# Forgetting attention: row maxima from a product with the queries in rows, subtracted inside the score product

## The chip, the cores and the metric

The kernel runs on one core of a Trainium2 chip. The metric is the device time of one execution in microseconds (us). TensorE (PE in the profile) multiplies matrices, VectorE (DVE) and ScalarE (ACT) work on elements, GpSimd (POOL) does a few fills, and SyncE (SP) issues the DMAs. TensorE writes to PSUM, in which the kernel keeps eight tiles ("banks" below) of 128 x 512 fp32; the other data lie in SBUF.

## The reference

One decoder layer on 2048 tokens of width 1024, in fp32: adaLN modulation, a combined input projection, sliding-window attention on 8 heads, forgetting attention on 8 heads of 64, an output projection, a gated MLP of width 2816 with a causal convolution, and a final norm. The change touches the forgetting attention:

```python
def forgetting_attention(q, k, v, f_logit):
    F = jnp.cumsum(jax.nn.log_sigmoid(f_logit.astype(jnp.float32)), axis=1)
    ...
    def one_block(args):
        qi, Fi, n = args
        s = jnp.einsum('bqhd,bkhd->bhqk', qi, k).astype(jnp.float32) * (HEAD_DIM ** -0.5)
        s = s + (Fi[..., None] - Fk[:, :, None, :])
        q_pos = n * BLOCK + jnp.arange(BLOCK)
        s = jnp.where(k_pos[None, :] <= q_pos[:, None], s, NEG)
        p = jax.nn.softmax(s, axis=-1)
        return jnp.einsum('bhqk,bkhd->bqhd', p.astype(v.dtype), v)
```

Each query has its own shift (the row maximum) in the softmax; any shift gives the same result as long as the exponentials stay in range.

## The kernel before

**Numbers.** A fp32 operand is split into a high part, rounded to the type fp32r that TensorE multiplies fast, and a low part that holds the rest. A dense product is three matmuls (high x high, high x low, low x high).

**Stages.** The tokens are cut into four blocks n = 0..3 of 512. For each block s1 projects the input, s2 does both attentions, and s3 does the output projection and the MLP. s2 is a side stream: `merge` weaves it into a main stream of dense products (s2(0) into s1(1) and s1(2); s2(1) into s3(0); s2(2) into s1(3) and s3(1); s2(3) into s3(2)); s3(3) is alone. Both streams yield costs in the planner's own microseconds; the side stream advances when its sum of costs lies behind the main one's, times a ratio (`RM`, `att_cost`), and when the last step lies far enough back (`GAPS`, `SGAPS`). Within what they write, a scheduler then orders each engine's queue. The engines take their queues in order.

**Forgetting attention before (`fox`, `fox_unit`).** Scores lie transposed: 128 keys in the partitions, queries in the columns. A unit is one head and 512 queries (blocks 0 and 1) or 256 queries (blocks 2 and 3: two key blocks then share a 512-column tile). `score` makes two matmuls for each key block: the stationary operand holds the keys' high and low parts one above the other in 128 rows, the moving one the query's high or low part twice. ScalarE copies the scores from PSUM to a tile `t` in SBUF and adds the keys' gate bias (L981); on the diagonal VectorE does it with the causal mask (L975). VectorE keeps a running maximum over key blocks (`keep_max`, L941, L947, L955). When all scores of a unit are there, `columns_max` transposes that maximum (L989) and reduces it (L991); `exps` spreads it over the partitions with transposes of a broadcast column (L996), copies it to SBUF (L1003), and then, for all tiles in a row, subtracts it on VectorE (L1010, L1014), takes the exponential on ScalarE (L1015), and adds up (L1022, L1025). `group` splits each tile into a high part `ph` on ScalarE (L724) and a low part `pl` on VectorE (L725); `pv` multiplies both with the values (L1059, L1062). `sums_of_rows` (L1035) and `over_rows` (L996) give the division by the row sums.

**Queues and buffers.** Three PSUM banks with the tag `s` carry the scores, all these transposes and those of sliding-window attention. SBUF tiles `t` (10), keys `kk` (6), values `vv` (5) and queries `q` (3) rotate. Weights are loaded on SP's queue, in one row with all other DMAs.

**The first weights.** At the very start `ada_pair` loads w_ada into tiles `t`; the rows of x lie in `ap`, 22 tiles `act`.

## Time and profile before

| | |
|---|---|
| median of 2 runs | 2647.84 us (2646.96 to 2648.71) |
| profiled execution | 2648.82 us, its span 2647.1 us |
| PE busy | 2541.4 us, 96% |
| PE weight loads busy | 2151.1 us, 81% |
| DVE busy | 1926.8 us, 73% |
| ACT busy | 1458.4 us, 55% |
| mean granted TensorE clock | 0.980 |
| DMA, mean share of the 16 engines | 66.3%, 588 MB |

The line numbers are those of the kernel before. A row of groups gives line, engine, operation, the names `out<-in`, shapes, count, busy time and the mean of one in ns, and then the engine's idle time before it with what ended it. A matmul's own duration includes its way through the array, so that successive ones overlap in the trace: the rate of TensorE is the distance from start to start. By the starts of their products (L964 to L847) the side stream's blocks lie here: s2(0) from 110 to 413 us, s2(1) from 416 to 920, s2(2) from 960 to 1602, s2(3) from 1593 to 2228, and after that there is only dense work.

### The profile page before, as it was taken

What the parts mean: (1) busy time and instruction counts of PE and PEld (TensorE: products, weight loads), DVE (VectorE), ACT (ScalarE), POOL (GpSimd) and SP (SyncE); (2) the same over time, 40 slices, a digit from 0 to 9 for tenths busy, and PEclk for the clock granted to TensorE, in tenths of its full rate; (3) what the DMA queues carried; (4) which work ended last, traced back from release to release, by engine and by line L of the source; (5) the groups of instructions that cost most, each with busy time, mean ns of one, the idle gap of its engine ahead of it and who ended that gap; (6) DMA issues with size and microseconds to landing.
All of it is one profiled execution on the core that took longest, in us unless ns stands there. A gap on an engine that the chain in (4) does not pass through costs nothing.

```text
span 2647.1 us, 38431 instructions
## 1 busy us (share of the span) xinstructions
PE 2541.4 (96%) x12852; PEld 2151.1 (81%) x12852; DVE 1926.8 (73%) x3837; ACT 1458.4 (55%) x3061; POOL 84.1 (3%) x171
## 2 busy tenths in 40 slices
PE   7999999799999999999999999999998999999998
PEld 5888888688887889878888878888886778888887
DVE  6468767899998668788888767878888787444433
ACT  4456665555667675575556665755555666412222
POOL 0001000100000010000000001000000000000000
PEclk9999999799999999999999999999998999999999
DMA  6967679576556976756666799555544477655564
GB/s 230 305 203 254 204 231 344 182 254 211 188 189 212 288 239 215 251 199 240 228 230 235 258 290 312 176 182 194 187 153 148 139 235 246 252 191 191 193 238 173
DMA packets 304770, 588.25 MB, mean 222 GB/s; under 512 B 32188, under 2 KB 137396, under 8 KB 304572
## 3 DMA queue, kind: packets, MB, share of 16 engines
q1 hardware_dynamic: 304572, 585.79, 66.3%
q8 instruction: 102, 1.67, 0.3%
q14 instruction: 96, 0.79, 0.1%
HBM read 440.95 MB, written 144.71 MB: 221 GB/s over the span
## 4 chain that ended last, share of the span: by engine, by line
PE 83%; DVE 6%; DMA 6%; ACT 2%; issue 1%; SPq 1%; POOL 0%; POOLq 0%; DVEq 0%; ACTq 0%
PE d L1297 36%; PE d L1179 21%; PE d L619 8%; PE s L964 4%; PE d L647 3%; PE o L1062 2%; PE o L1059 2%; DVE t L1010 1%; DMA wada<-in_w_ada_dram 1%; PE d L282 1%; DMA q<-qd 1%; PE s L794 1%; PE mb L996 1%; PE pt L836 1%; DVE pl L725 1%
## 5 line engine op out<-in xcount | busy, mean ns | idle before, releaser
L1297 PE MATMUL d<-hh,wkh 128*128 128x512 f32 (+1 forms) x920 | 351.3, 384 | 3.3 <-ACT hh L115 1.6
L1297 PE MATMUL d<-hl,wkh 128*128 128x512 f32 (+1 forms) x920 | 353.2, 385 | 0.1
L1297 PE MATMUL d<-hh,wkl 128*128 128x512 f32 (+1 forms) x920 | 351.7, 383 | 0.0
L384 ACT CAST wh<-wr 128x1024 fp32r<-128x1024 f32 (+5 forms) x184 | 188.7, 1027 | 162.4 <-PE d L1297 72.0
L385 DVE TENSOR_TENSOR wl<-wr,wh 128x1024 fp32r<-128x1024 f32 (+5 forms) x184 | 219.0, 1191 | 80.0 <-ACT wh L384 78.4
L981 ACT ACTIVATE t<-s,bc 128x256 f32<-128x256 f32 (+3 forms) x464 | 201.1, 483 | 124.7 <-PE s L964 70.6
L1327 ACT ACTIVATE u<-d,cb,cw 128x512 f32<-128x512 f32 x176 | 136.3, 778 | 192.9 <-PE d L1297 179.8
L1330 DVE SCALAR_TENSOR_TENSOR u<-d,cw,u 128x511 f32<-128x511 f32 x176 | 130.4, 743 | 153.6 <-ACT u L1327 152.8
L724 ACT CAST ph<-t 128x512 fp32r<-128x512 f32 (+2 forms) x304 | 177.1, 591 | 110.0 <-PE o L1059 109.6
L1297 PE MATMUL d<-hh,wh 128*128 128x512 f32 (+1 forms) x552 | 211.1, 385 | 0.4 <-ACT hh L115 0.4
L1297 PE MATMUL d<-hh,wl 128*128 128x512 f32 (+1 forms) x552 | 211.0, 383 | 0.2 <-DVE wl L385 0.2
L1297 PE MATMUL d<-hl,wh 128*128 128x512 f32 (+1 forms) x552 | 211.0, 383 | 0.0
L725 DVE TENSOR_TENSOR pl<-t,ph 128x512 fp32r<-128x512 f32 (+2 forms) x304 | 192.9, 645 | 24.7 <-ACT ph L724 24.5
L964 PE MATMUL s<-q,kkb 128*128 128x256 f32 (+2 forms) x1024 | 197.0, 311 | 14.0 <-ACT t L981 5.9
L1297 PEld LDWEIGHTS d<-hh,wkh 128*128 128x128 f32 x920 | 173.2, 189 | 35.4 <-DVE halo L1341 2.2
L1297 PEld LDWEIGHTS d<-hh,wkl 128*128 128x128 f32 x920 | 173.9, 189 | 31.5
L1297 PEld LDWEIGHTS d<-hl,wkh 128*128 128x128 f32 x920 | 173.9, 189 | 30.9 <-DVE hl L530 0.5
L1015 ACT ACTIVATE t<-t 128x512 f32<-128x512 f32 (+2 forms) x304 | 170.3, 603 | 11.6 <-DVE t L1014 8.5
L964 PEld LDWEIGHTS s<-q,kkb 128*128 128x128 f32 x1024 | 153.8, 197 | 26.8 <-ACT t L981 8.2
L1062 PE MATMUL o<-pl,vvb 128*128 128x256 f32 (+2 forms) x512 | 148.8, 310 | 18.2 <-DVE pl L725 18.0
L1059 PE MATMUL o<-ph,vvb 128*128 128x256 f32 (+2 forms) x512 | 151.5, 311 | 8.2 <-ACT ph L724 6.2
L619 PE MATMUL d<-hh,wh 128*128 128x512 f32 x360 | 142.5, 399 | 6.6 <-DVE lf L662 4.0
(233 smaller groups left out, 6061.9 us busy)
## 6 DMA issues: line engine op xcount, KB each, us to landing
wkh<-wsu SPq DMA_DIRECT2D x110, 512.0 KB, 3.3
wkl<-wsu SPq DMA_DIRECT2D x110, 512.0 KB, 4.2
wr<-in_w_up_dram SPq DMA_DIRECT2D x66, 512.0 KB, 5.4
wkh<-wsd SPq DMA_DIRECT2D x55, 512.0 KB, 4.0
wkl<-wsd SPq DMA_DIRECT2D x55, 512.0 KB, 4.2
wada<-in_w_ada_dram SPq DMA_DIRECT2D x96, 256.0 KB, 5.8
wr<-in_w_in_c_dram SPq DMA_DIRECT2D x45, 512.0 KB, 4.6
wsu<-wh SPq DMA_DIRECT2D x44, 512.0 KB, 2.9
```

The source lines that it names most:

```text
L384: nc.scalar.copy(wh, raw)
L385: nc.vector.tensor_sub(wl, raw, r32(wh))
L619: nc.tensor.matmul(ps, a[:, k, :], b[k], start=(k == 0 and i == 0), stop=(k == KT - 1 and i == 2),)
L724: nc.scalar.copy(ph[:, e0:], src[:, e0:])
L725: nc.vector.tensor_sub(pl[:, e0:], src[:, e0:], r32(ph[:, e0:]))
L964: nc.tensor.matmul(ps[:, o + low(c0) : o + w], st["kks"][kb // 4][:, (kb % 4) * P : (kb % 4 + 1) * P], qs[a][:, low(c0) : w], start=(a == ...
L981: nc.scalar.activation(tt[:, plain : o + w], ps[:, plain : o + w], AF.Identity, bias=bias(kb))
L1015: nc.scalar.activation(t1, t1, AF.Exp)
L1059: nc.tensor.matmul(po[:, c:], v, ph[:, o + c : o + w], start=(kb == 0), stop=False)
L1062: nc.tensor.matmul(po[:, c:], v, pl[:, o + c : o + w], start=False, stop=(kb == nkb - 1))
L1179: nc.tensor.matmul(acc[t], l[:, ts], r[:, k % 2, :], start=(i == 0 and l is ah and r is wh), stop=(i == n_k - 1 and l is al),)
L1297: nc.tensor.matmul(ps[:, c], w[a][:, k, :], b[k][:, c], start=(k == 0 and i == 0), stop=(k == KT - 1 and i == 2),)
```

## The change

**Units.** All blocks use units of 512 queries; each key block has its own tile. Two products replace the two of before and a new one is added.

**Row maxima (`highest`, `shift_rows`).** For each unit, each group of 128 queries u and each block m of up to 512 keys, one matmul gives the scores with the queries in the partitions. It has 68 rows: 64 of the high parts of query and key, and four of ones on the query's side against two rows of ones and the gate bias's high and low part on the keys' side (`b_d`, new, made in `sums_of_gates`: the bias is transposed on TensorE, split, and stored to DRAM by four DMAs for each block). So it holds the score plus bias plus 2. VectorE reduces it straight from PSUM; on the diagonal it adds a mask first. `shift_rows` combines these, adds an offset between blocks (`offs`), takes 2 minus the maximum, splits that, transposes it to two rows, and ScalarE writes them under the low part of the query (`qx`).

**Scores and exponentials.** `score` is again two matmuls: keys (high above low) times the query's high part, and 66 rows with the keys' high part and two rows of ones times the query's low part and the two shift rows. So the maximum is subtracted in PSUM, and ScalarE takes the exponential from PSUM with the gate bias as its bias. On the diagonal VectorE adds bias and mask first. There is no running maximum, no subtraction and no spreading of the maximum. A tile is summed (`acc`) as soon as it is there. `group(kb)` now emits the scores of key block kb+1 and the split of block kb.

**Buffers and the planner.** Tiles `t` go from 10 to 6 (three of them for sliding-window scores), `kk` from 6 to 10, `q` from 3 to 5. `ada_pair` takes its tiles from `act`. The costs in `att_cost` rise, and units of forgetting attention are started one unit ahead. The products for the maxima (`pm`) and the scores (`s`) share the three PSUM banks with the tag `s`.

```diff
@@ sums_of_gates
+            pb = dense_ps()[: 4 * NH, :P]
+            nc.tensor.transpose(
+                pb, bc[:, 4 * n : 4 * n + 4, :].rearrange("p t h -> p (t h)"), ident
+            )
...
+            nc.scalar.copy(bt[:, 2, :], pb)
+            nc.vector.tensor_sub(bt[:, 3, :], pb, r32(bt[:, 2, :]))
+            for t in range(4):
+                nc.sync.dma_start(
+                    b_d[n][:, :, t * P : (t + 1) * P], r32(bt[t * NH : (t + 1) * NH, :, :])
+                )
@@ fox, setup
+            nc.sync.dma_start(r32(q1[0:HD, :]), q_d[n][0, r0 : r0 + HD, :])
+            for m in range(n + 1):
+                kx = at.tile([P, TB], F32R, tag="kk", name="kx", bufs=KB)
+                nc.sync.dma_start(r32(kx[0:HD, :]), k_d[m][0, kr : kr + HD, :])
+                nc.sync.dma_start(r32(kx[HD : HD + 4, :]), b_d[m][h])
+                st["kxs"].append(kx)
...
@@ fox_unit
+        def highest(u, m):
...
+            w = TB if m < n else max(256, (u + 1) * P)
+            ps = pa.tile([P, 512], F32, tag="s", name="pm", bufs=3)
+            nc.tensor.matmul(
+                ps[:, :w], st["q1"][0 : HD + 4, u * P : (u + 1) * P],
+                st["kxs"][m][0 : HD + 4, :w], start=True, stop=True,
+            )
+            mc = sm["mc"]
+            if m < n:
+                nc.vector.tensor_reduce(mc[:, u, m : m + 1], ps, AX.X, ALU.max)
+                return
+            junk = tp.tile([P, P], F32, tag="t", name="mjunk")
+            nc.vector.tensor_tensor_reduce(
+                out=junk, in0=ps[:, u * P : (u + 1) * P], in1=qmask, scale=1.0,
+                scalar=-BIG, op0=ALU.add, op1=ALU.max, accum_out=mc[:, u, n : n + 1],
+            )
+            if u > 0:
+                nc.vector.tensor_reduce(
+                    sm["md"][:, u : u + 1], ps[:, : u * P], AX.X, ALU.max
+                )
+        def shift_rows():
...
+            nc.vector.tensor_reduce(top, mc[:, :, : n + 1], AX.X, ALU.max)
...
+            nc.vector.tensor_scalar(top, top, -1.0, 2.0, ALU.mult, ALU.add)
+            nc.vector.tensor_copy(nh, top)
+            nc.vector.tensor_copy(nm[:, :, 0], r32(nh))
+            nc.vector.tensor_sub(nm[:, :, 1], top, r32(nh))
+            ps = pa.tile([P, 512], F32, tag="s", name="nt", bufs=3)
+            for u in range(4):
+                nc.tensor.transpose(ps[0:2, u * P : (u + 1) * P], nm[:, u, :], ident)
+            nc.scalar.copy(st["qx"][HD : HD + 2, :], ps[0:2, :])
+        def score(kb):
...
+            nc.tensor.matmul(
+                ps[:, c:], st["kks"][kb // 4][:, ks], st["qa"][:, c:], start=True, stop=False
+            )
+            nc.tensor.matmul(
+                ps[:, c:], st["kxs"][kb // 4][0 : HD + 2, ks], st["qx"][0 : HD + 2, c:],
+                start=False, stop=True,
+            )
...
+                nc.scalar.activation(tt[:, plain:], ps[:, plain:], AF.Exp, bias=bias(kb))
...
-        def exps():
-            mm = at.tile([P, 512], F32, tag="mm", name="mm", bufs=MMB)
-            nc.scalar.copy(mm[:, :w], over_rows(sm["m"])[:, :w])
-            for g, parts in enumerate(steps):
...
-                    adder(SD, "sub").tensor_tensor(
-                        t2, t2, mm[:, None, :w].to_broadcast([P, 2, w]), ALU.subtract
-                    )
...
-                nc.scalar.activation(t1, t1, AF.Exp)
...
+        def group(kb):
+            if kb == 0:
+                score(0)
+            if kb + 1 < nkb:
+                score(kb + 1)
+            c = low(kb)
+            ph, pl = split(tts.pop(kb), c)
@@ s2 and att_cost
-        free = NT
+        free = NT - 3
...
-        return MRG * (44.0, 72.0, 97.0, 124.0)[n]
+        return MRG * (51.0, 86.0, 121.0, 156.0)[n]
```

**How the queues change.** VectorE's queue at a change of units in block 3, before, in the middle of w_up's work (`u`, `act` and `halo` belong to the MLP):

```order
L1330 SCALAR_TENSOR_TENSOR u<-d,cw_1138,u 128x511
L1040 TENSOR_REDUCE rl<-lt 128x2
L1010 TENSOR_TENSOR t<-t,mm 128x512 x7
L1333 SCALAR_TENSOR_TENSOR u<-d,cw_1128,u 128x510
L1338 TENSOR_TENSOR u<-u,halo 128x2
L941 TENSOR_TENSOR mx<-t 128x512
L1044 RECIPROCAL rl<-rl 128x2
L1022 TENSOR_TENSOR acc<-t 128x512
```

And now, where a unit of block 3 begins (`mc<-pm` reduces a product for the maxima of the next unit):

```order
L971 TENSOR_REDUCE mc<-pm 128x1
L754 TENSOR_TENSOR pl<-t,ph 128x512
L1033 TENSOR_TENSOR acc<-t 128x512
L1345 SCALAR_TENSOR_TENSOR halo<-d,cw_1147,halo 128x1
L754 TENSOR_TENSOR pl<-t,ph 128x512
L1036 TENSOR_TENSOR acc<-acc,t 128x512
L1077 TENSOR_TENSOR yo<-yo,mb 64x512
L754 TENSOR_TENSOR pl<-t,ph 128x512
L971 TENSOR_REDUCE mc<-pm 128x1
```

The seven subtractions in a row are gone; one reduction stands in each step in their place.

TensorE's queue at the same change of units in block 3, before (`d` are dense products, `mt` and `mb<-ident,m` the transposes for the maximum, `lt` those for the row sums):

```order
L989 MATMUL mt<-ident,mx 128x128 x2
L964 MATMUL s<-q,kkb 128x256 x4
L1297 MATMUL d<-hh,wkl 128x512
L996 MATMUL mb<-ident,m 128x128 x2
L964 MATMUL s<-q,kkb 128x256 x4
L1035 MATMUL lt<-ident,acc 128x128 x2
L964 MATMUL s<-q,kkb 128x256 x8
L1059 MATMUL o<-ph,vvb 128x256
L1297 MATMUL d<-hh,wkh 128x512
```

And now, in the middle of a unit of block 3:

```order
L965 MATMUL pm<-kx,q_17982 128x512
L1301 MATMUL d<-hh,wkh 128x512
L1301 MATMUL d<-hl,wkh 128x512
L1071 MATMUL o<-ph,vvb 128x512
L1301 MATMUL d<-hh,wkl 128x512
L1301 MATMUL d<-hh,wkh 128x512
L1011 MATMUL s<-qa,kkb 128x512
L1014 MATMUL s<-qx,kx 128x512
L1301 MATMUL d<-hl,wkh 128x512
L1072 MATMUL o<-pl,vvb 128x512
```

Every step now fills two banks with the tag `s`, one with a product for the maxima and one with the two for the scores, and carries two products of 512 columns with the values; dense products stand between.

TensorE's queue at the gates of block 0, now (`d<-ident,bc` is the new transpose of the bias):

```order
L626 MATMUL d<-hl,wh 128x512
L626 MATMUL d<-hh,wl 128x512
L683 MATMUL d<-lf,tri 128x32
L683 MATMUL d<-lf,ones 128x32
L709 MATMUL d<-ident,bc 32x128
L626 MATMUL d<-hh,wh 128x512
```

The transpose stands directly behind the gate sums, from which VectorE first has to make `bc`. In block 1, 2 and 3 some attention products stand between.

More of the change, by code (lines that the diff above doesn't have):

```diff
@@ L41 @@
 HOOKS = (13, 17, 20)
-KB = 6
+KB = 10
 VB = 5
@@ L49 @@
 MY = 1
-QB = 3
+QB = 5
 MXB = 2
@@ L986, in columns_max @@
-        def columns_max():
-            ps = pa.tile([P, 4, P], F32, tag="s", name="mt", bufs=3)
-            for u in range(nj):
-                nc.tensor.transpose(ps[:, u, :], sm["mx"][:, u * P : (u + 1) * P], ident)
-            sm["m"] = sp.tile([P, 4], F32, tag="m", name="m")
-            nc.vector.tensor_reduce(sm["m"][:, :nj], ps[:, :nj, :], AX.X, ALU.max)
-        def over_rows(c):
+                    mc[:, :, :n], mc[:, :, :n],
+                    offs[n][:, None, :, h].to_broadcast([P, 4, n]), ALU.add,
+                )
@@ L1044, in sums_of_rows @@
-            nc.vector.reciprocal(rl[:, :nj], rl[:, :nj])
-        def group(g):
-            c = low(steps[g][0][2]) if per == 1 else 0
-            ph, pl = split(tts[g], c)
+            for u in range(4):
+                nc.tensor.transpose(ps[:, u, :], sm["acc"][:, u * P : (u + 1) * P], ident)
+            rl = sm["rl"] = sp.tile([P, 4], F32, tag="rl", name="rl")
+            nc.vector.tensor_reduce(rl, ps, AX.X, ALU.add)
+            nc.vector.reciprocal(rl, rl)
+        def group(kb):
[5 more added lines that the diff above has]
+            ph, pl = split(tts.pop(kb), c)
+            if kb == nkb - 1:
+                sums_of_rows()
```

256 lines of the change are left out of this document (105 added, 151 removed).

## The prediction

> **What bounds the kernel now.** I read the page first, then the windows, the waits, and the timeline at the places that these name.
>
> ```profile
> PE 2541.4 (96%) x12852; PEld 2151.1 (81%) x12852; DVE 1926.8 (73%) x3837; ACT 1458.4 (55%) x3061; POOL 84.1 (3%) x171
> ...
> PE 83%; DVE 6%; DMA 6%; ACT 2%; issue 1%; SPq 1%; POOL 0%; POOLq 0%; DVEq 0%; ACTq 0%
> ```
>
> TensorE is busy 96% of the span and holds 83% of the chain that ended last. Matmuls overlap in the trace, so a busy share is no rate. The windows give the rate, and show where TensorE stands idle (columns: stretch, length, then busy us and instructions of each engine, granted clock, DMA share, GB/s).
>
> ```profile
> 0.00:100.00 100.00, 82.48 (x396) 70.83 (x397) 56.73 (x105) 42.12 (x74) 6.27 (x19) 0.97 0.73 243
> ...
> 400.00:500.00 100.00, 86.44 (x381) 69.13 (x379) 85.39 (x151) 49.10 (x90) 9.05 (x9) 0.87 0.95 326
> ...
> 600.00:700.00 100.00, 100.00 (x463) 82.03 (x462) 92.71 (x168) 57.23 (x105) 0.57 (x2) 1.00 0.60 202
> ...
> 1900.00:2000.00 100.00, 88.20 (x466) 75.08 (x465) 83.05 (x167) 57.63 (x126) 0.61 (x3) 0.93 0.50 164
> 2000.00:2100.00 100.00, 89.10 (x461) 75.74 (x459) 83.96 (x160) 57.55 (x123) 0.82 (x4) 0.93 0.47 151
> ...
> 2300.00:2400.00 100.00, 100.00 (x443) 82.82 (x442) 40.66 (x72) 20.49 (x28) 0.00 (x0) 1.00 0.56 200
> ```
>
> At 2300 us all work is dense, in products of 512 columns: 100 us / 443 = 0.226 us each. At 600 us, in the middle of s2(1), VectorE is at 93% and TensorE still has no gap. So where attention runs evenly beside dense work, work taken from VectorE buys nothing and work given to TensorE is paid in full. The gaps lie in a few places (13.6 us in the window at 400, 11.8 at 1900, 10.9 at 2000), and there the granted clock is 0.87 to 0.93. The waits say for whom (us in total, times, longest):
>
> ```profile
> PE o L1062 <- DVE pl L725: 18.0, 16, 3.7
> ...
> PE o L1059 <- ACT ph L724: 6.2, 4, 3.2
> PE s L964 <- ACT t L981: 5.9, 6, 1.8
> ...
> PE mb L996 <- ACT t L1015: 5.2, 1, 5.2
> ...
> PE s L964 <- DVE yo L1070: 3.5, 1, 3.5
> PE lt L1035 <- DVE acc L1025: 3.3, 1, 3.3
> ```
>
> These six belong to forgetting attention and make 42.1 us. The timeline of the three engines at a change of units in block 3 (start, us):
>
> ```profile
> 1905.09 0.28 PE L1062 MATMUL o<-pl,vvb 128*128 128x256 f32 x1
> 1905.21 0.28 PE L1059 MATMUL o<-ph,vvb 128*128 128x256 f32 x1
> ...
> 1914.23 0.38 PE L989 MATMUL mt<-ident,mx 128*128 128x128 f32 x2
> 1914.36 0.71 PE L964 MATMUL s<-q,kkb 128*128 128x256 f32 x4
> ...
> 1921.87 0.58 PE L1059 MATMUL o<-ph,vvb 128*128 128x256 f32 x1 [3.24 <-ACT ph L724]
> 1923.77 0.80 PE L1297 MATMUL d<-hh,wkh 128*128 128x512 f32 x1 [1.31 <-DVE halo L1341]
> ```
>
> ```profile
> 1917.10 4.29 DVE L1010 TENSOR_TENSOR t<-t,mm 128x512 f32<-128x512 f32 x7
> ```
>
> ```profile
> 1919.07 2.25 ACT L1015 ACTIVATE t<-t 128x512 f32<-128x512 f32 x4
> ```
>
> Seven subtractions hold VectorE for 4.29 us, the exponentials follow, and TensorE's in-order queue has the first product with them ahead of dense work: 3.24 and 1.31 us idle.
>
> **The change on TensorE.** Prices from start to start: 0.226 us for 512 columns, 0.12 for 256 (from 1905.09 to 1905.21), 0.173 for 384 as the middle, 0.065 for a transpose (two from 1914.23 to 1914.36). The products before:
>
> ```profile
> L964 PE MATMUL s<-q,kkb 128*128 128x256 f32 x896 | 152.8, 295 | 9.4 <-ACT t L981 4.1 <-DVE yo L1070 3.5 <-DVE pl L725 1.6
> ...
> L1059 PE MATMUL o<-ph,vvb 128*128 128x256 f32 x448 | 124.6, 296 | 6.2 <-ACT ph L724 6.2
> ...
> L964 PE MATMUL s<-q,kkb 128*128 128x512 f32 x96 | 35.9, 448 | 4.6 <-DVE mod L219 2.6 <-ACT t L981 1.8 <-DMA q<-qd 0.2
> ```
>
> With 32 of 384 columns, counted in the code, the scores cost 896 x 0.12 + 96 x 0.226 + 32 x 0.173 = 134.7 us. With one tile for each key block they are 448 of 512, 64 of 384 and 128 of 256: 127.7 us. The products with the values have the same counts, so both together save 14.0. New are the products for the maxima: for each of 8 heads and each n, 4n + 1 of 512 columns, one of 384 and two of 256, so 224 x 0.226 + 32 x 0.173 + 64 x 0.12 = 63.8 us. Of the transposes 256 go (L989, and half of L996) and 128 narrow ones come, at 0.065 or less: -8.3, at most -16.6. The sum on TensorE is 63.8 - 14.0 - 8.3 = **+41.5 us**. No trace shows a product with 66 or 68 rows; I price it like one with 128, the nearest row, and take another price as a rival.
>
> **The change on VectorE and ScalarE.**
>
> ```profile
> L1010 DVE TENSOR_TENSOR t<-t,mm 128x512 f32<-128x512 f32 x208 | 128.0, 684 | 18.0 <-ACT mm L1003 18.0
> L947 DVE TENSOR_TENSOR mx<-mx,t 128x512 f32<-128x512 f32 x168 | 114.2, 680 | 1.4
> ...
> L955 DVE TENSOR_TENSOR mx<-mx 128x256 f32<-128x256 f32 x32 | 13.3, 416 | 0.3
> ...
> L991 DVE TENSOR_REDUCE m<-mt 128x4 f32<-128x512 f32 x16 | 11.0, 688 | 2.7 <-PE mt L989 2.7
> ```
>
> ```profile
> L981 ACT ACTIVATE t<-s,bc 128x256 f32<-128x256 f32 (+3 forms) x464 | 201.1, 483 | 124.7 <-PE s L964 70.6
> ...
> L1015 ACT ACTIVATE t<-t 128x512 f32<-128x512 f32 (+2 forms) x304 | 170.3, 603 | 11.6 <-DVE t L1014 8.5
> ```
>
> The subtractions go: 256 of 512 columns at 0.684 and 48 narrower ones at some 0.46, 197 us. The running maxima go: 208 at 0.68, 80 narrower ones, and 48 reductions, some 201 us. In come 192 reductions of 512 columns at 0.688, 96 narrower ones at 0.42, 128 masked ones of 128 columns at 0.34 (all by the rows above or their slope, from 0.42 at 256 to 0.68 at 512), and eight small operations for each of 32 units at 0.16: 132 + 40 + 44 + 41 = 257 us. VectorE is relieved by about 140 us. A reduction is no dearer here than an elementwise pass, 0.688 against 0.680. The Trainium skill (VectorE: DVE Perf Modes, Rules for kernel authors) calls the reduction the slowest operation of this engine and advises another structure; by that the 132 us would be more, by the trace they are not. ScalarE loses 464 x 0.483 = 224 us and keeps its exponentials, a bit longer from PSUM (about +40 with a second one on the diagonal): some -180 us.
>
> Almost all of that relieves engines which nobody waits for. What it can buy is bounded by the 42.1 us of waits above and by the clock that is missing after them, 13 + 7 + 7 = 27 us in the three windows with gaps. For a place between none and all I count the queue. Before, 42 of 288 score groups follow the one before with no dense product between, and there VectorE needs 4 x 0.68 us against 8 x 0.12 on TensorE, 1.76 us too much: 74 us, of which 42 are seen as waits. Now it is 60 of 320, with 3 x 0.68 against 5 x 0.226, 0.92 too much: 55 us. By that ratio 11 us of waits go. The bursts of subtractions, which hold a whole unit up, go entirely, so that is too little; I take half of the waits, 21 us, and 4 of the clock: **-25 us**. What is late next is the chain from a score to its split, which stays.
>
> **The small parts.** The new transpose of the gate bias waits for VectorE's chain behind the gate sums. Before:
>
> ```profile
> 125.68 0.39 PE L676 MATMUL d<-lf,ones 128*128 128x32 f32 x2
> ```
>
> ```profile
> 127.84 0.16 DVE L683 TENSOR_TENSOR bc<-bc,tot 128x8 f32<-128x8 f32 x1
> ```
>
> The chain ends 2.1 us after the sums have left TensorE. In block 0 nothing stands between in the new queue and the dense products behind it wait too; in the others 4 to 20 products stand there. I take +3, between 0 and 4 x 2.1 = 8. In the prologue the loads of w_ada now need a free `act` tile:
>
> ```profile
> 9.00 0.42 PE L517 MATMUL sd<-ident,xrow 128*128 128x128 f32 x1
> ```
>
> ```profile
> 5.71 5.39 SPq L200 DMA_DIRECT2D wada<-in_w_ada_dram  x8
> ```
>
> The sixth, issued at about 5.71 + 5 x 0.67 = 9.1, now waits for the transposes that end at 9.4, and the weights queued behind it on SP with it: +1, between 0 and 3. The page's line on DMA:
>
> ```profile
> DMA packets 304770, 588.25 MB, mean 222 GB/s; under 512 B 32188, under 2 KB 137396, under 8 KB 304572
> ```
>
> Loads and stores for `kx` and the bias add 157 issues and some 11 MB (10 of 131 KB and 8 KB for each head) to these 588; on SP's queue weight loads now stand behind `kx` loads that wait for a key tile. I cost that at nothing, because weights are fetched three products ahead; without that cover 157 x 0.67 us of issue would lie ahead of L1297. Three tiles instead of ten for sliding-window scores spread those units out; dense products stand between, so nothing, and without them up to the 11 us that such a window is idle now, in each block.
>
> **The sum.** 2648.82 (the profiled execution, 1.7 us above its span, 1.0 above the median) + 41.5 + 3 + 1 - 25 = 2669, against the median some **2668 us**, +0.8%. Its own range goes from all waits and clock gained, 2694 - 69 = 2625, to none gained and the upper ends of the small parts, 2700.
>
> **The rivals.** *Slower: the banks.* Three `s` banks now take two fillings for each key block, one emptied by VectorE. If the 55 us above come as waits, with the old 42 replaced by them, the time is 2694 + 13 = 2707; with both, 2749; the middle is 2728. Against it speaks that such steps needed more of VectorE before; for it, that there are more of them. It decides from 7 us more of waits than today, since 2701 is +2%, about what a measurement of this kernel can tell from no change. Chance 0.20.
>
> *Slower: a drain.* A matmul's own time against the rate:
>
> ```profile
> L1297 PE MATMUL d<-hh,wkh 128*128 128x512 f32 x840 | 329.8, 393 | 1.5 <-DVE halo L1341 1.5
> ```
>
> If TensorE had to run empty before each of the 640 products with 66 or 68 rows, each would cost 0.393 - 0.226 = 0.167 us more: 107 us, 2776. Nothing in this trace mixes row counts outside the prologue. The Trainium skill (TensorEngine Tiling (Array Packing), Key Properties) says that a change of tiling mode drains TensorE; it counts row tiling only up to 64 rows, and by that it would not happen here. Chance 0.05.
>
> *Faster.* If shorter queues on VectorE and ScalarE also empty the waits of dense work, the bound is all idle time behind the prologue, 105.7 - 17.5 = 88 us, and the clock, 2% of 2541 = 51 us: 2555; with three quarters 2590. Against it: windows with VectorE at 93% have no gap. Chance 0.07.
>
> **How the numbers follow.** My forecast has 0.68; 0.04 of that lies above 2701. So faster by over 2% has 0.07, within 2% 0.64, slower 0.29. The range from 2612 to 2738 holds the forecast and the first rival up to its middle.
>
> **What would show it.** Right: in the window that is only dense the rate is still 0.226; products for the maxima lie 0.226 apart; VectorE falls to about 1790 us and ScalarE to about 1280; the bursts at changes of units are gone, and the waits for `pl` and `ph` are about half. Wrong: waits of `pm` or `s` for a reduction or an exponential (banks), 66-row products more than 0.3 us apart beside full ones (drain), or a window beside w_up that loses idle time that it has not got.

## The result, and the profile after

| | before | after |
|---|---|---|
| median | 2647.84 us | 2728.02 us (2724.43 to 2731.61, 2 runs) |
| ratio, 95% interval | | 1.030 (1.027 to 1.033) |
| profiled execution, its span | 2648.82, 2647.1 us | 2724.43, 2722.5 us |
| mean granted TensorE clock | 0.980 | 0.973 |

The change makes the kernel 3.0% slower. The page of the changed kernel, its engines and the chain that ended last:

```profile
PE 2609.0 (96%) x12280; PEld 2161.9 (79%) x12280; DVE 1809.1 (66%) x3959; ACT 1327.7 (49%) x2697; POOL 72.4 (3%) x148
...
PE 82%; DMA 6%; DVE 6%; ACT 3%; issue 1%; SPq 1%; POOL 0%; POOLq 0%; DVEq 0%; ACTq 0%
```

VectorE lost 118 us and ScalarE 131 us of work, and TensorE is still busy 96% of a longer span. The windows say where it stands idle now (columns as before: stretch, length, PE, PEld, DVE, ACT, POOL busy, granted clock, DMA share, GB/s). First the kernel before at 200 us, then the changed kernel:

```profile
200.00:300.00 100.00, 98.69 (x570) 87.36 (x569) 80.72 (x188) 69.55 (x144) 10.94 (x22) 1.00 0.70 224
```

```profile
200.00:300.00 100.00, 91.39 (x504) 80.78 (x504) 71.65 (x227) 56.52 (x126) 6.09 (x16) 0.93 0.71 225
400.00:500.00 100.00, 89.20 (x360) 69.86 (x359) 70.39 (x182) 47.32 (x103) 0.00 (x0) 0.86 0.85 289
600.00:700.00 100.00, 100.00 (x455) 81.82 (x455) 88.22 (x177) 52.73 (x93) 0.41 (x2) 1.00 0.63 213
2000.00:2100.00 100.00, 93.58 (x400) 74.64 (x399) 71.62 (x151) 47.07 (x87) 0.41 (x2) 0.95 0.54 169
2200.00:2300.00 100.00, 89.41 (x423) 72.26 (x422) 60.44 (x152) 66.60 (x168) 0.21 (x1) 0.94 0.67 211
2270.00:2300.00 30.00, 19.41 (x88) 14.21 (x87) 17.23 (x58) 24.60 (x70) 0.00 (x0) 0.80 0.36 101
2400.00:2500.00 100.00, 100.00 (x443) 82.80 (x442) 42.54 (x77) 20.38 (x28) 0.00 (x0) 1.00 0.56 198
```

Dense work alone runs as before (443 products in 100 us), and so does the middle of s2(1) at 600 us. At 2000 us the gaps are smaller than before (6.4 us against 10.9). New are the gaps at 200 us, in block 0, where scores wait for the masked maxima (`md`) at 230 and 279 us, and a stretch of 30 us at 2270 with 10.6 us idle and a clock of 0.80. TensorE's waits (us in total, times, longest):

```profile
PE pt L865 <- ACT tsw L115: 11.3, 4, 6.1
PE o L1072 <- DVE pl L754: 11.2, 11, 2.9
PE o L876 <- DVE yo L893: 8.4, 4, 3.5
PE o L876 <- ACT ph L753: 7.9, 4, 3.6
...
PE s L1011 <- DVE md L979: 4.7, 3, 2.3
PE s L1011 <- ACT t L1028: 3.5, 4, 1.7
PE nt L1003 <- DVE nm L1000: 2.7, 2, 2.4
...
PE d L709 <- DVE bc L690: 2.2, 1, 2.2
PE pm L965 <- DMA kx<-kd: 2.0, 2, 1.4
```

The wait for `pl` fell from 18.0 to 11.2 us. In its place stand waits of **sliding-window** products (L865, L876), 27.6 us in three rows; before, the largest row of theirs was this:

```profile
PE o L847 <- DVE yo L864: 1.7, 2, 1.2
```

For the books I price each TensorE product by the start-to-start time of its width (0.2265 us for 512 columns, 0.173 for 384, 0.119 for 256, 0.068 for a transpose, between the 0.03 and the 0.11 us that most of them take, 0.150 and 0.147 for the narrow V products) and call what its successor starts later than that a **gap**: idle time and lost clock together, booked at the product ahead of the late one. Summed over every start in each trace, as price + gap in us:

| products | before | after | `swa_six` | `no_max_six` |
|---|---|---|---|---|
| for the maxima | | 63.9 + 27.9 | 63.9 + 28.9 | |
| fox scores | 133.9 + 35.4 | 127.8 + 20.1 | 127.8 + 17.9 | 127.8 + 19.2 |
| fox with the values | 133.9 + 56.8 | 127.8 + 36.4 | 127.8 + 36.2 | 127.8 + 21.5 |
| fox transposes | 34.8 + 13.3 | 26.1 + 8.2 | 26.1 + 8.2 | 17.4 + 9.7 |
| sliding window | 75.4 + 20.2 | 75.4 + 43.0 | 75.4 + 33.0 | 75.4 + 29.5 |
| projections of s1 | 358.6 + 9.3 | 358.6 + 23.0 | 358.6 + 20.9 | 358.6 + 15.4 |
| s3's dense products | 1611.0 + 43.7 | 1611.0 + 45.9 | 1611.0 + 39.2 | 1611.0 + 34.0 |
| prologue, gates, row transposes of all blocks (L517, now L524) | 65.8 + 43.5 | 66.1 + 50.0 | 66.1 + 45.4 | 66.1 + 45.1 |
| sum | 2413.5 + 222.3 | 2456.7 + 254.5 | 2456.7 + 229.7 | 2384.1 + 174.3 |

(The last two columns are experiments, below; "fox" is forgetting attention.) Of the 75.4 us between the two spans 43.2 are products and 32.2 are gaps. Fox's old products lost 41 us of gaps, but those for the maxima brought 28, sliding-window products 23, the projections 14 and the prologue's row 6.5.

### The profile page after: what moved, and what is told of

The parts are those of the page before. It is cut to its first block, busy times and chain, and to the rows that moved or that the text cites. A ratio compares the mean times of both kernels' runs of the same rounds, so it can differ in the third digit from the quotient of the medians.

```text
span 2722.5 us, 37017 instructions
## 1 busy us (share of the span) xinstructions
PE 2609.0 (96%) x12280; PEld 2161.9 (79%) x12280; DVE 1809.1 (66%) x3959; ACT 1327.7 (49%) x2697; POOL 72.4 (3%) x148
## 2 busy tenths in 40 slices
DMA packets 307066, 599.56 MB, mean 220 GB/s; under 512 B 33660, under 2 KB 129140, under 8 KB 306876
## 4 chain that ended last, share of the span: by engine, by line
PE 82%; DMA 6%; DVE 6%; ACT 3%; issue 1%; SPq 1%; POOL 0%; POOLq 0%; DVEq 0%; ACTq 0%
PE d L1301 35%; PE d L1183 21%; PE d L626 8%; PE d L654 2%; PE s L1011 2%; PE o L1072 2%; PE s L1014 2%; PE pm L965 2%; PE o L1071 2%; DMA wada<-in_w_ada_dram 1%; PE d L288 1%; DMA yd<-yo 1%; DVE pl L754 1%; PE s L823 1%; PE d L524 1%
## 5 line engine op out<-in xcount | busy, mean ns | idle before, releaser
L1028 ACT ACTIVATE t<-s,bc 128x512 f32<-128x512 f32 (+3 forms) x288 | 175.1, 612 | 154.1 <-PE s L1014 153.5
L754 DVE TENSOR_TENSOR pl<-t,ph 128x512 fp32r<-128x512 f32 (+1 forms) x320 | 195.3, 617 | 5.8 <-ACT ph L753 4.9
L753 ACT CAST ph<-t 128x512 fp32r<-128x512 f32 (+1 forms) x320 | 178.5, 568 | 21.8 <-PE o L1071 9.8
L1036 DVE TENSOR_TENSOR acc<-acc,t 128x512 f32<-128x512 f32 (+2 forms) x256 | 154.8, 605 | 47.5 <-ACT t L1028 45.0
L971 DVE TENSOR_REDUCE mc<-pm 128x1 f32<-128x512 f32 x192 | 130.5, 685 | 72.0 <-PE pm L965 71.1
L626 PE MATMUL d<-hl,wh 128*128 128x512 f32 x360 | 144.1, 401 | 0.0
L626 PE MATMUL d<-hh,wl 128*128 128x512 f32 x360 | 143.0, 398 | 0.0
L1011 PE MATMUL s<-qa,kkb 128*128 128x512 f32 (+1 forms) x320 | 123.0, 385 | 12.2 <-DVE md L979 4.7
```

Of the source, the lines that this page charges most:

```text
L626: nc.tensor.matmul(ps, a[:, k, :], b[k], start=(k == 0 and i == 0), stop=(k == KT - 1 and i == 2),)
L753: nc.scalar.copy(ph[:, e0:], src[:, e0:])
L754: nc.vector.tensor_sub(pl[:, e0:], src[:, e0:], r32(ph[:, e0:]))
L1011: nc.tensor.matmul(ps[:, c:], st["kks"][kb // 4][:, ks], st["qa"][:, c:], start=True, stop=False)
L1028: nc.scalar.activation(tt[:, plain:], ps[:, plain:], AF.Exp, bias=bias(kb))
L1036: nc.vector.tensor_add(ac, ac, tt[:, c:])
```

## The experiments

Each is compared with the kernel before, run beside it on the same chip; ratios are to it, and us are medians.

### The tiles for sliding-window scores

Two views of block 3's end in the changed kernel. The timeline from 2274 us (start, duration):

```profile
2274.84 0.40 PE L876 MATMUL o<-ph,vva 128*128 128x512 f32 x1
...
2275.18 0.50 PE L877 MATMUL o<-pl,vva 128*128 128x512 f32 x1
...
2277.17 1.69 ACT L115 ACTIVATE tsw<-tsw,ls 128x256 f32<-128x256 f32 x4
2277.72 0.69 PE L865 MATMUL pt<-ident,tsw 128*128 128x128 f32 x2 [2.04 <-ACT tsw L115]
2278.06 1.20 PE L823 MATMUL s<-kka,q 128*128 128x256 f32 x4
```

No dense product stands there: the units run one behind the other, each from its scores to ScalarE's exponentials and its transposes. By the starts of their products the four stretches in which sliding-window attention runs after fox took 74 + 81 + 76 + 53 = 284 us before and 95 + 104 + 91 + 64 = 354 us now.

```diff
+                    if i == n_fox:
+                        free += 3      # swa_six: all six tiles once fox is done
```

> The changed kernel, but sliding-window units may use all six tiles `t` once the last unit of forgetting attention of a block is done, and three before that, as now. Theory 'three tiles': the 23 us more of gaps around the sliding-window products (43.0 us against 20.2 before) and some of the 10 us around the dense products beside them come from three tiles; 2728 falls by 20 to 33 us, to 2695 to 2708, and in block 3 the stretch with sliding-window products alone (2272 to 2300 us) is gone. Rival 'late start': the side stream simply comes 39 to 75 us later than before and meets the end of the dense work whatever its tiles; the time stays within 6 us of 2728 and that stretch stays.

2701.3 us, ratio 1.019 (1.017 to 1.021): 27 us less than the change. The four stretches take 82 + 78 + 77 + 51 = 288 us again, and total gaps fall by 24.8 us. The end of block 3 shrinks, but does not go (windows):

```profile
2240.00:2260.00 20.00, 20.00 (x106) 16.84 (x105) 13.37 (x43) 18.28 (x55) 0.00 (x0) 1.00 0.80 226
2260.00:2280.00 20.00, 14.10 (x65) 10.28 (x64) 14.25 (x38) 15.67 (x41) 0.00 (x0) 0.83 0.41 127
```

The same limit put into the kernel before:

```diff
+        swa_free = 3
...
-                if free >= 1 and ahead:
+                if free >= 1 and ahead and (j < n_fox or swa_free >= 1):
```

> The kernel before, but with at most three tiles `t` for sliding-window scores, nothing else changed. Theory 'three tiles': the same loss appears without any of the rest of the change, 2648 + 20 to 33 = 2668 to 2681. Rival 'late start': before, the units lie early enough that dense products stand between, and the time stays within 6 us of 2648.

2668.0 us, ratio 1.006 (1.004 to 1.008): 16 us, where 20 to 33 were expected. Sliding-window gaps go from 20.2 to 31.7 us, and the wait that leads the changed kernel's list appears here too (a row of TensorE's waits):

```profile
PE pt L836 <- ACT tsw L115: 7.8, 4, 4.2
```

So three tiles cost 16 us by themselves and 27 us in the changed kernel, presumably because its units come later and meet less dense work.

```diff
-NT = 6
+NT = 8        # and the small tiles 9 -> 7; all eight once fox is done
```

> The changed kernel with eight tiles `t` in place of six (two of the nine small temporary tiles given up), five of them for sliding-window scores while forgetting attention runs and all eight after. With three and then six of six it was 2701. Theory 'three tiles': the 12.8 us of gaps around sliding-window products that this left over the kernel before go as well, 2686 to 2696. Rival: what is left belongs to the later start of each block's attention, and the time stays within 5 us of 2701.

2705.8 us, ratio 1.022 (1.020 to 1.024): no gain over six, though two small tiles were given up for it. Nothing here says that what is left of the sliding-window gaps is a matter of tiles.

### The price of the maxima, taken apart

The steps of the planner stay, and the parts are put back one at a time. The shift is the query's own gate bias from DRAM, so the runs that leave the shift rows out, or do not read them, compute something else and measure time alone.

```diff
-            "scores": [(highest, (u, m), 0.23) for m in range(n + 1) for u in range(4)],
-            "turns": [(shift_rows, TAS[n])],
+            "scores": [(lambda: None, (), 0.23) for _ in range(4 * n + 4)],
+            "turns": [(lambda: None, TAS[n])],
```

> The changed kernel without the row maxima: the 320 products `pm`, their reductions and the 128 transposes of the shift rows are left out, the planner's steps and costs stay. The shift is the query's own gate bias, read from DRAM, and fox's queries are scaled by 1/64 in place of 1/8 so that exponentials stay in range (so the output is another one). Theory 'paid in full, banks harmless': the products go with their ideal price, 63.9 + 8.3 = 72 us, and the gaps stay: 2656. Theory 'banks': the gaps around `pm` (27.9 us) and some of those around `s` go too: 2610 to 2630.

2588.7 us, ratio 0.977 (0.975 to 0.979): the maxima cost 139 us, twice their price on TensorE. Between the two traces it is 129 us, 72.6 of price and 56.4 of gaps.

With the six tiles on top (the diff of `swa_six`):

> The run without maxima (2589) with six tiles `t` for late sliding-window units. Theory 'the terms add': the 27 us of the tiles go here too, 2556 to 2568, and what the change gains when neither the maxima nor the tiles are paid is 80 to 92 us against the kernel before. Rival 'the tiles' loss was made by the maxima': without them the units come early enough, 2582 to 2595.

2571.7 us, ratio 0.970 (0.968 to 0.972), a little above the range: the tiles cost 17 us here. This is the change without its two losses, 79 us faster than the kernel before, and no usable kernel: its shift is not the maximum.

Only the products put back (`highest` without its reductions, no shift rows, `kx` and `q1` loaded as in the change):

> The run without maxima (2589) with the 320 products `pm` put back, but nothing reads them: reductions, shift rows and their transposes stay left out. The maxima as a whole cost 139 us, of which the products and transposes are 72 by their ideal price and some 60 are gaps. Theory 'what waits for the reductions': the gaps come from the bank that each reduction holds, from VectorE's queue or from the chain to the shift rows; here they stay away and the products cost their price or less, 2615 to 2657. Theory 'TensorE's own queue': the products bring their gaps with them wherever they stand, 2680 to 2720.

2656.9 us, ratio 1.0025 (1.0007 to 1.0042): 68 us for a price of 63.9. As expected of products that nobody reads.

Only the reductions, out of SBUF:

```diff
+            ps = r32(st["kks"][m])     # no product; the reductions read the keys' tile
```

> The run without maxima (2589) with the 448 reductions put back on VectorE, but reading the keys' tile in SBUF, with no product and no shift rows: VectorE's load without TensorE's and without the banks. Theory 'VectorE's queue': split tiles `pl` and the MLP's operations stand behind reductions, and 20 to 55 of the 60 us of gaps are back: 2609 to 2644. Theory 'banks': VectorE has room at some 66%, and the time stays within 8 us of 2589.

2623.3 us, ratio 0.991 (0.989 to 0.994): 35 us. The gaps of this trace exceed those without maxima by 36 us: 12 at sliding-window products, 11 at the row transposes (L524) and 6.5 at the scores, and only 2 us of the 36 lie ahead of 110 us.

Products and reductions, without the shift rows:

> The changed kernel with its products for the maxima and their reductions straight from PSUM, but the results are not used: the shift rows are left out (eight small operations on VectorE and four transposes for each unit), and the score takes the query's own gate bias from DRAM in their place, with queries scaled by 1/64 as in the run without maxima. So far 2589 without maxima, +68 for unread products, +35 for reductions from SBUF, which leaves 36 of the 139 us. Theory 'banks': these 36 come from reductions that hold the banks; only the 8 us of transposes and the small operations go, 2712 to 2722. Theory 'chain to the shift rows': scores wait at each start of a unit for the last maximum, and that goes: 2685 to 2700.

2690.7 us, ratio 1.0165 (1.0145 to 1.0185). That is 34 us over the unread products, as much as the reductions out of SBUF: these runs show no cost of the PSUM bank that a reduction holds. And it is 37 us below the change: the shift rows cost more than the banks that I suspected, although their transposes are 8.7 us by price. Three runs take them apart. VectorE's small operations alone:

> The run without shift rows (2691) with only VectorE's seven or eight small operations for each unit put back; the transposes and ScalarE's copy stay left out. Theory 'VectorE's queue': some 41 us of small operations hold up the split tiles and reductions behind them, 2703 to 2725. Theory 'transposes and their bank': 2685 to 2697, and the cost comes only with the transposes.

2683.6 us, ratio 1.012 (1.010 to 1.014): 7 us less than without them, so no cost. The whole chain, copied to a tile that nobody reads:

```diff
-            nc.scalar.copy(st["qx"][HD : HD + 2, :], ps[0:2, :])
+            nc.scalar.copy(sink[HD : HD + 2, :], ps[0:2, :])
```

> The run without shift rows (2691) with their whole chain put back, the small operations on VectorE, the four transposes into an `s` bank and ScalarE's copy out of it, but the copy goes to a tile that nobody reads; the scores still take the gate bias from DRAM. Theory 'dependence': scores wait for the shift rows; only the 8.7 us of transposes come back, 2696 to 2704. Theory 'VectorE and banks': the chain's own work costs it, whoever reads it, 2716 to 2732.

2727.9 us, ratio 1.029 (1.027 to 1.031): the full cost, so the scores' dependence on the maxima is not what costs. A row of ScalarE's waits in this trace led to a new suspect: its copy stands at the head of its queue until TensorE reaches the transposes:

```profile
ACT sink L1006 <- PE nt L1004: 109.9, 27, 12.8
```

The chain without that copy:

> The run with the unread shift rows (2728) without ScalarE's copy out of PSUM: VectorE's small operations and the four transposes for each unit stay, nobody reads their bank. VectorE's operations alone made 2684. Theory 'ScalarE': the copy stands at the head of ScalarE's queue until TensorE has reached the transposes (110 us in 27 waits in that run), and exponentials behind it are late; without it only the 8.7 us of transposes remain, 2688 to 2700. Theory 'TensorE's queue': the transposes wait for VectorE's chain and hold up what is behind them, 2715 to 2732.

2733.6 us, ratio 1.031 (1.030 to 1.033): ScalarE is cleared, the transposes bring it. Yet TensorE hardly waits for them (a row of its waits):

```profile
PE nt L1004 <- DVE nm L1001: 3.5, 2, 3.2
```

Against VectorE's operations alone the gaps are 40.6 us larger, 17 of them at the products with the values. The copy on VectorE, in the version with six tiles:

```diff
-            nc.scalar.copy(st["qx"][HD : HD + 2, :], ps[0:2, :])
+            nc.vector.tensor_copy(st["qx"][HD : HD + 2, :], ps[0:2, :])
```

> The run with six tiles for late sliding-window units (2701), the shift rows copied out of PSUM by VectorE in place of ScalarE. Theory 'ScalarE': its 48 us of waiting for the transposes go and exponentials come sooner, 2670 to 2690, unless VectorE loses as much in its place. Theory 'TensorE's queue': within 6 us of 2701.

2712.3 us, ratio 1.024 (1.022 to 1.026), 11 us more than with ScalarE: VectorE is the worse place.

### Where the transposes cost: the order at the ends of units

The timeline of the changed kernel at the end of a unit in block 3, VectorE and TensorE:

```profile
2043.74 0.74 DVE L1334 SCALAR_TENSOR_TENSOR u<-d,cw,u 128x511 f32<-128x511 f32 x1
2044.02 0.41 PE L1071 MATMUL o<-ph,vvb 128*128 128x384 f32 x1
2045.40 0.29 DVE L974 CUSTOM_DVE_ANT_0 mjunk<-pm,qmask 128x128 f32<-128x128 f32 x1
...
2045.62 0.55 DVE L979 TENSOR_REDUCE md<-pm 128x1 f32<-128x384 f32 x1
2046.09 0.74 DVE L1334 SCALAR_TENSOR_TENSOR u<-d,cw,u 128x511 f32<-128x511 f32 x1
2046.75 0.55 DVE L754 TENSOR_TENSOR pl<-t,ph 128x384 fp32r<-128x384 f32 x1
2047.35 0.69 PE L1072 MATMUL o<-pl,vvb 128*128 128x384 f32 x1 [2.92 <-DVE pl L754]
```

The masked maxima of the next unit, its second reduction and the MLP's `u` stand before `pl` on VectorE, and TensorE waits 2.92 us. In this unit and the one before, no dense product lies between the products of the last four key blocks; their gaps are 7.2 and 4.7 us. In the two runs with reductions but without the transposes (`no_shift`, `shift_dve`) 44 to 46 and 41 dense products lie there, with gaps of 0.3 to 0.4 us. One number of the planner, its delay ahead of the shift rows in block 3, changes that and leaves the transposes in:

```diff
-TAS = [1.5, 3, 4, 2]
+TAS = [1.5, 3, 4, 4]     # with six tiles
```

> The run with six tiles for late sliding-window units (2701), with the planner's delay before the shift rows in block 3 raised from 2 to 4. By the written order, two of that block's eight units no longer end with their last four key blocks in one row without a dense product between (0 and 0 dense products before, 42 and 48 now). Theory 'order at the ends of units': the gaps at these two places (4.7 and 7.2 us in the changed kernel) and the clock lost after them go, 2676 to 2692. Rival: the gaps belong to the transposes as such, wherever they stand; within 6 us of 2701.

2689.3 us, ratio 1.016 (1.014 to 1.018), 12 us less than with six tiles alone (9 us by the ratios). 48 and 42 dense products lie at these two places now, and their gaps are 0.1 and 0.3 us: 11.5 of the 13.6 us by which all gaps fall between the two traces. The window of the earlier place with six tiles alone, and here:

```profile
1900.00:2000.00 100.00, 96.05 (x422) 77.95 (x421) 70.91 (x151) 44.20 (x82) 0.20 (x1) 0.97 0.54 173
```

```profile
1900.00:2000.00 100.00, 100.00 (x451) 82.21 (x451) 71.79 (x150) 43.18 (x78) 0.20 (x1) 1.00 0.56 179
```

So 9 to 12 of the 37 to 50 us are shown to be order. That the absence of dense products is the exact condition is not: in the run with unread shift rows 20 and 26 of them lie there and the gaps are 6.8 and 5.8 us. The rest of the transposes' cost is spread over the blocks and stays open; no run separates the bank that they take from their place in the queue.

### Banks, doubled products, and three attempts to do better

One of the three `s` banks given to the products for the maxima alone:

```diff
-            ps = pa.tile([P, 512], F32, tag="s", name="pm", bufs=3)
+            ps = pa.tile([P, 512], F32, tag="pm", name="pm", bufs=1)   # and two banks "s"
```

> The changed kernel with one of the three `s` banks given to the products for the maxima alone; scores, transposes and sliding-window products share the other two. Theory 'order in the banks': scores wait because the bank whose turn it is holds a product for the maxima that VectorE has not reduced yet; with a bank of their own the scores come free of it, and the time falls by 5 to 20 us from 2728. Theory 'too few banks': what counts is their number; each product for the maxima now waits for the reduction of the one before, and the time rises by 10 to 40 us.

2825.9 us, ratio 1.068 (1.065 to 1.071), worse than any theory gave. Products for the maxima now wait for the reduction before them, 40 us in these two of TensorE's rows:

```profile
PE pm L965 <- DVE md L979: 22.3, 24, 1.8
...
PE pm L965 <- DVE mc L971: 17.9, 13, 2.9
```

And the gaps at sliding-window products, which have two banks left, go from 43.0 to 84.8 us. The number of banks matters a great deal; that three shared ones are already too few does not follow, and a fourth was not tried.

```diff
+            for _ in range(2):      # pm_twice: the same product again into the same bank
                 nc.tensor.matmul(
```

> The changed kernel with each product for the maxima made twice into the same bank; nothing else differs in what is computed. Theory 'paid in full, banks harmless': 63.9 us more, 2792, within 6. Theory 'banks': the three banks are held longer in each step and the waits of `s` and `pm` grow with it, 2800 to 2825. If some of TensorE's time beside the side stream were free, less than 50 us more.

2754.4 us, ratio 1.039 (1.037 to 1.041): 26 us more for 63.9 us of products. Both main theories are wrong, and "less than 50 us more" holds. Gaps fell by 30 us. That TensorE had free time there is not shown all the same: 14 of the 30 us are at the products with the values, and 11 of these at the two ends of units named above, where 54 and 46 dense products stand in this run and the gaps are 0.2 and 0.4 us. The second products changed the order too, so this run is no clean price of a product.

```diff
-                nc.vector.tensor_add(ac, ac, tt[:, c:])
+                nc.gpsimd.tensor_tensor(ac, ac, tt[:, c:], ALU.add)   # with six tiles
```

> The run with six tiles for late sliding-window units (2701), with 224 of the additions to the row sums (`acc`, 0.605 us each on VectorE, some 140 us) moved to GpSimd, which is 3% busy. Theory 'VectorE's queue': the gaps that the reductions bring through VectorE (35 us) shrink, 2670 to 2692. Theory 'banks alone': the time stays within 6 us of 2701. If GpSimd is so much slower that the tiles `t` and the row sums at a unit's end wait for it, the time rises by 10 to 60 us.

2699.3 us, ratio 1.019 (1.018 to 1.021): nothing. But it does not show that relief of VectorE is worth nothing, since VectorE was hardly relieved: 256 additions left it (the expectation has 224), and its busy time fell only from 1807.4 to 1782.0 us, as other operations took longer. The split `pl` with six tiles alone, and here (a row of each page):

```profile
L754 DVE TENSOR_TENSOR pl<-t,ph 128x512 fp32r<-128x512 f32 (+1 forms) x320 | 196.1, 619 | 6.0 <-ACT ph L753 4.8
```

```profile
L754 DVE TENSOR_TENSOR pl<-t,ph 128x512 fp32r<-128x512 f32 (+1 forms) x320 | 253.9, 799 | 38.6 <-ACT ph L753 37.2
```

```diff
-GAPS = [1.5, 1.5, 1.2, 1.5]
+GAPS = [1.5, 1.5, 1.2, 1.3]     # with six tiles
```

> The run with six tiles for late sliding-window units (2701), with the least spacing of attention steps in block 3 lowered from 1.5 to 1.3 of the planner's microseconds, so that the block's attention ends before the dense work beside it does. Theory 'late start': the last 20 us of sliding-window work without dense products beside it (2260 to 2280 us, 11.5 us of gaps) are covered, and the time falls by 6 to 13 us to 2688 to 2695. Rival: denser steps bring as many gaps in the middle of the block, within 5 us of 2701.

2735.3 us, ratio 1.033 (1.032 to 1.035): 34 us slower. Sliding-window gaps fall (33.0 to 27.8 us), but the middle of the block pays: from 1800 to 2200 us TensorE is busy 370.0 us in place of 388.2. The same window with six tiles alone, and here:

```profile
2000.00:2100.00 100.00, 92.26 (x392) 72.52 (x392) 74.73 (x173) 46.49 (x89) 0.41 (x2) 0.95 0.52 164
```

```profile
2000.00:2100.00 100.00, 89.57 (x365) 70.41 (x365) 70.91 (x168) 41.61 (x83) 0.20 (x1) 0.88 0.45 144
```

The shift rows by DMA through DRAM in place of transposes:

```diff
-                nc.tensor.transpose(ps[0:2, u * P : (u + 1) * P], nm[:, u, :], ident)
...
+                nc.gpsimd.dma_start(n_d[h][n][a].rearrange("(u p) -> p u", u=4), nm[:, :, a])
+            nc.gpsimd.dma_start(r32(st["qx"][HD : HD + 2, :]), n_d[h][n])
```

> The run with six tiles for late sliding-window units (2701), the shift rows brought from columns to rows by DMAs through DRAM on GpSimd's queue (two stores of 512 values in pieces of 4 bytes, one load), with no transpose and no copy on ScalarE. If the terms add, the 37 to 44 us of transposes and copy go: 2656 to 2672. If the DMAs take longer than the planner's five microseconds from the shift rows to the first score, scores stand at the head of TensorE's queue: 2710 to 2760.

3224.2 us, ratio 1.217 (1.215 to 1.219). A wait row of TensorE, and a row of the DMAs (operation, count, size, median us from issue to landing):

```profile
PE s L1016 <- DMA qx<-nd: 429.6, 31, 27.9
```

```profile
nd<-nm POOLq DMA_DIRECT2D x64, 2.0 KB, 10.4
```

Two stores of 10.4 us and a load of 2.5 us, one after the other: each unit's first score waits 14 us on average at the head of TensorE's queue. None of the versions that keep the maxima beats the kernel before; the best, with six tiles and the later shift rows, is 1.6% slower.

## Why the prediction was right or wrong

**The time.** 2728 lies in the range, but 60 us above the forecast of 2668: 80 us slower than before where 20 were forecast. In the terms of the sum, against the spans: forecast +41.5 + 3 + 1 + 0 - 25, measured +43.2 for products and +32.2 for gaps.

**Products: right.** +43.2 against +41.5; put back alone, those for the maxima cost 68 us against 63.8. A product with 66 rows costs what one with 128 costs (start to start 0.233 against 0.231 us in the median, 0.234 with 68 rows), so the rival *drain* is out. The Trainium skill (TensorEngine Tiling (Array Packing), Available Configurations) lists row tiling with at most 64 rows in a tile; the trace agrees that nothing drains at 66 and 68. That each such product is paid in full is shown where nobody reads it; doubled in the changed kernel, the run grew by 0.4 of their price only, with another order in its queue.

**VectorE and ScalarE: nearly right, and beside the point.** VectorE fell to 1809 us, not 1790: the subtractions were 176 us by their rows (128.0 + 48.4), where I put 197. The new reductions of 512 columns cost what I took (groups by shape, with an addition of two tiles for comparison):

```profile
L971 DVE TENSOR_REDUCE mc<-pm 128x1 f32<-128x512 f32 x192 | 130.5, 685 | 72.0 <-PE pm L965 71.1
...
L1036 DVE TENSOR_TENSOR acc<-acc,t 128x512 f32<-128x512 f32 x168 | 115.0, 685 | 41.5 <-ACT t L1028 40.8
```

130.5 us against 132; at 685 ns a reduction out of PSUM is no slower than the addition of two tiles, so by the trace the Trainium skill's advice against reductions (VectorE: DVE Perf Modes, Rules for kernel authors) does not bear here. ScalarE fell to 1328, not 1280: the row of the copies has 201.1 us, while I multiplied its mean by its count to 224, and the shift rows' copies (18.4 us) were not in the sum.

**The relief of 25 us: the step that failed, from both sides.** "I take half of the waits" was too little for what is removed: without the maxima and the tiles' loss, gaps fall by 48.0 us (222.3 to 174.3), and the run is 79 us faster. It was wrong that nothing comes in its place. The sentence "The bursts of subtractions, which hold a whole unit up, go entirely" is true, but at the ends of two units of block 3 there is a new burst, where the next unit's masked maxima meet the last key blocks. By the table the gaps' +32.2 us are -48.0 for what is removed, +55.4 for the maxima (`no_max_six` to `swa_six`) and +24.8 for the tiles. The maxima's gaps by parts, between medians beyond the price: 4 us with the products, 34 with the reductions, 29 with four small transposes for each unit (-2, 29 and 30 between the traces). I had costed the reductions as VectorE's time only, at nothing because VectorE was relieved on balance, and had put the transposes into a sum of widths. The queue count in the prediction (55 us in place of 74) looked at `s` fillings, the wrong place: by the rows of waits, `pm` and `s` wait 8 us in all for a reduction (`md`, `mc`), half of it in block 0. Nor did it count alike on both sides: without a dense product between, 72 of 304 score groups follow the one before in the trace before and 69 of 320 after (the prediction: 42 of 288 and 60 of 320); 42 and 25 follow directly.

**Three sliding-window tiles at nothing: the second step that failed.** The cover named there ("dense products stand between") is not given by the queue: with three tiles a unit's steps must follow each other, the stretches grow by 70 us, and in block 3 the dense work ends before them. Its price is 27 us in the changed kernel, 17 without the maxima, 16 in the kernel before. The prediction's own bound, up to 11 us in each block, would have held it.

**Gates, prologue, DMAs: small, but the gates are dearer than their wait.** The new transpose waits 2.2 us once (L709), as the chain of 2.1 us had said. But just ahead of it the gate sums of block 0 wait 3.9 us for VectorE's `lf` (0.6 before), and the clock falls (1.00 before and 0.87 now from 110 to 150 us): between 115 and 145 us the gaps go from 2.4 to 10.1 us, against +3 and a bound of 8. In the other traces with the new transpose they are 4.5 to 10.9 us. Gaps ahead of 110 us go from 29.4 to 30.1 us, against +1. The waits of `pm` for `kx` are 2.0 us, and 599.56 MB are 11.3 more than before, against some 11.

**The banks.** The rival's middle, 2728, is the measured time, but by chance: reductions out of banks cost 34 us and out of SBUF 35, and 27 of the 60 us of the miss are the sliding-window tiles, which it did not contain.

**The signs.** The rate of dense work and the halved waits of forgetting attention for `pl` and `ph` (24.2 to 11.8 us) were as forecast. What the signs left out are the units that the change does not rewrite, but whose buffers it takes.

## What to carry to other kernels

A change that hands buffers from one stage to another has a price in the stage that gives them up; cost it from the length of that stage's chain and from the dense work that is left beside it, not from the average. On a kernel whose busiest engine takes its queue in order, an operation's time on an idle engine says little: ask instead what stands behind it at the places where steps bunch, the ends of units above all. Taking parts out and putting them back one at a time, with the planner's steps kept, gave each part its price (68, 34 and 37 of 139 us), where the rows of waits had twice pointed at the wrong part (the banks, ScalarE). Such a price holds to some ten us at best, because a changed order alone moves a run by that much: VectorE's small operations came out at -7 us. And when work is moved to another engine, read afterwards whether the first one was relieved.

## What the runs showed of the hardware that was not expected

- Short gaps cost clock as well. From 2270 to 2300 us no wait of TensorE is longer than 2.75 us, and the granted clock of that window is 0.80, where dense work has 1.00. The Trainium skill (TensorE: Matmul & The Clock Gate, What's actually happening) says that the clock falls after an idle window of about 3.4 us; here a row of shorter gaps is enough.
- A store of 512 values of 4 bytes from 128 partitions on GpSimd's queue lands 10.4 us after its issue, the load of 4 KB back 2.5 us after.
- Additions on GpSimd made VectorE's operations longer: the mean of the split `pl` rose from 619 to 799 ns when 256 additions moved to GpSimd. In that trace a `pl` of 512 columns takes 1.10 us in the mean where an addition on GpSimd overlaps it (120 of them) and 0.68 where none does (104).
